# A hybrid attention layer on one core: the norm's row sent through DRAM, later places for copies and forget logits, two new banks at the end, and gate units placed anew

## Chip, core and metric

The kernel runs on one core of one Trainium2 chip. The metric is the device time of one execution in microseconds (us). TensorE is called PE here, VectorE DVE, ScalarE ACT, GpSimd POOL, and SyncE SP; SP issues most of the DMAs, and its own queue is SPq in the profile.

## What is computed

One layer over 512 frames of width 2048, in float32:

```python
hn = rmsnorm(x, norm_g)                          # x * rsqrt(mean(x*x)+eps) * g
proj = hn @ w_in                                 # 2048 -> 3*(q,k,v,gate of 512) + 4 + 3*2048
f_logit = proj[..., QKVG:QKVG+4] + b_f           # 4 forget logits a frame
gates = sigmoid(proj[..., QKVG+4:] + b_gate)     # three merge gates of width 2048
ya = forgetting_attention(rms(qa), rms(ka), va, f_logit)   # logits + c[t] - c[s], c = cumsum(log_sigmoid)
yb = chunked_relpos_attention(rms(qb), rms(kb), vb, rel_bias)
yc = stick_breaking_attention(qc, kc, vc)
ys = stack(ya, yb, yc) * silu(gate branches)
out = x + sum_n(gates_n * (ys_n @ w_up_n)) @ w_out
```

## The kernel before, in words

**Arithmetic.** A product of two float32 matrices is made of three passes in a shorter float format: each operand is split into a high part (ACT's copy, L249 in the profile) and a low part (DVE's subtraction, L253), and high*high, high*low and low*high are accumulated in a PSUM bank. The two large projections are done by a Strassen scheme with seven products (1 to 7) in place of eight; sums of weight blocks are made by DVE (L662, L668, L903 for values) and by adding DMAs that POOL issues.

**Units.** The work of PE is a list of units. A unit loads a block of weights (512 KB, SP), ACT and DVE split it (tile `w`, three buffers), and PE multiplies it with the split activations. One unit of a pair takes PE 2.8 us. First come the units of the first quad (q, k, v and gate of head C0, four banks at once), then the values of branch C (`value_units`, 14 units: product 1 in two halves, then product 2 in two halves, and so on), then head after head: `HEADS` lists for each head which units come between its q and k and the next head: `s` a pair of silu gates, `v` the 14 value units of the next branch, `g` a pair of merge gates. At the end come the up projection and the output projection (`OutTask`, twice).

**Order.** The kernel writes its instructions in an order that a planner in the kernel (`Flow`) works out while it is built. Each task is a generator that yields what it needs: an engine and a cost, an event, or a free buffer. The planner keeps one clock for each engine and always takes the task that can start first, then the one that is due first. `set_(event)` gives an event the end of the step that was placed last (`Flow.set`: `event.t = self.fin`). Data that a DMA brings is planned by `landing()`, at a rate that `line` adds up, plus 1.5; transposing DMAs by `XLATE`. On PE, ACT and DVE the order is kept as written, so an instruction whose data are late holds up all that stand behind it on its engine. SP's DMAs are kept in order too.

**The norm.** The projections run on x * g without the norm. `square_x` sums squares while x comes in; `norm_x` makes rsqrt of the mean as a column: `rcol`, 128 partitions by 4. The outputs have frames along the free dimension, so the factor is needed as a row of 512 in every partition: `rstd`, kept in `begin_in` (the buffer of the first tile of x). Before, `norm_x` makes four diagonal blocks `dg` from the identity (L527, ACT), multiplies them by a matrix of ones on PE (L532), and copies the bank to `rstd` (L536, ACT). `by_norm` (L544, DVE) multiplies a result by `rstd`. The first users are `f` (the forget logits' bank, `take_f`) and `c` (C0's v and k).

**Other places.** `forget_bias` reads the logits back as 128x64 (`lf_parts`, SP), adds them on DVE (L978) and computes log-sigmoid in short steps (L981 to L997). `Head.value` reads a head's values back from DRAM (`vr<-vd`) and splits them (`vh`, `vl`). `silu` reads a gate back. `together` copies a transposed block (`tt`) to 32-bit words (L1193, ACT). `OutTask.mms` gives PE the output products; `result` (L1846, DVE) adds a bank to the output tile `o`, which is stored. For the last unit (product 4, last quarter) the second block of rows is done in a left and a right half of 256 columns of one bank.

Of the kernel before, what the change touches and what calls it, by code (L numbers as in the profile page):

```python
# [163 lines left out]
def hybrid_kernel(  # L164
# [350 lines left out]
    def norm_x():  # L515

        m, tmp = small_n[:, 2, :], [small_n[:, i, :] for i in range(3, 6)]
        yield DVE, 0.2
        nc.vector.tensor_reduce(m, ssq, axis=AX.X, op=ALU.add)
        yield from rsqrt(rcol, m, D, tmp, 4)  # L520
        yield DVE, 0.1
        nc.vector.tensor_scalar_mul(rcol_s, rcol, SCALE)
        yield t2s, 1
        dg = t2("dg")
        for b in range(QB):
            yield ACT, 0.3
            nc.scalar.activation(dg[:, blk(b)], identf, AF.Copy, scale=rcol[:, b:b + 1])  # L527
        yield Event(flow.fin + 3.0)
        yield atts, 1
        ps = att()  # L530
        yield PE, 0.9
        nc.tensor.matmul(ps, onef, dg, start=True, stop=True)  # L532
        give(t2s, 2)
        yield begin_free
        yield ACT, act_us(S)
        nc.scalar.activation(rstd[0], ps, AF.Copy)  # L536
        give(atts)
        set_(rstd_ev)

    def by_norm(c, src=None):  # L540
# [425 lines left out]
    def forget_bias():  # L966
# [5 lines left out]
        yield f_ev  # L972
        yield from queued(nc.sync.dma_start, parts,
                          fd.rearrange("(n h) (c t) -> n (h c) t", h=NH, t=T).rearrange("n c t -> c n t"))
        yield Event(f_ev.t + 6.0)
        q = 0.15
        yield DVE, 2 * q
        nc.vector.tensor_reduce(v, parts.rearrange("p n t -> p t n"), axis=AX.X, op=ALU.add)  # L978
        nc.vector.tensor_scalar_add(v, v, bfc)
# [31 lines left out]
    class Head:  # L1011
# [249 lines left out]
        def value(self):  # L1261
            g, d = self.h // 2, self.h % 2
            task = values[self.n]
            for s in range(2):
                yield task.kept[g][s]
            for j in range(3):
                yield self.event("hl", j)
            yield t2s, 1
            t = t2("vr")
            to = t.rearrange("p (i s d) -> p i s d", i=2, s=2)  # L1270
            for s in range(2):
                ev = yield from fetch(to[:, :, s, :],
                                      task.dram[g][s].rearrange("p (i h d) -> p i h d", i=2, h=2)[:, :, d, :], 128)
            yield ev
            yield t2s, 2
            self.v = pair_of("v")
            yield from split(*self.v, t, S, self.event("v"))
            give(t2s)

        def silu(self):  # L1280

            if (self.n, self.h) in gd:
                d, ev = gd[self.n, self.h]
                yield ev
                yield t2s, 1
                g = t2("g")
                yield (yield from fetch(g, d, 256))
            else:
                yield self.event(G)
                g = self.c[G]  # L1290
                yield from by_norm(g)
# [181 lines left out]
    def first_head(n, h):  # L1473
        hd = Head(n, h)
        units.extend(first_quad(hd))
        at(OFF["fb"], forget_bias)
        value_units(n)
        gate_units()
        schedule(hd, OFF["a0"], OFF["b0"])
# [211 lines left out]
    class OutTask:  # L1691
# [94 lines left out]
        def mms(self, u):  # L1786
# [14 lines left out]
                        yield accs[i], 1  # L1801
                        self.ps[p, s] = acc(i)

            def step(s, part, cols):
                for j in range(QK):
                    k = kq * QK + j
                    yield lambda: mops[p](k) is not None
                    r, _, ev = mops[p](k)
                    yield ev
                    yield PE, mm_us(cols.stop - cols.start)  # L1810
                    w = u.lo if part == 1 else u.hi
                    mm(self.ps[p, s][:, cols], r[:, part // 2, s * P:(s + 1) * P], w[:, j, cols],
                       onto is None and kq + j + part == 0, kq == 3 and j == QK - 1 and part == 1, True)
# [14 lines left out]
            yield u.ready  # L1828
            for s in range(2):
                yield from step(s, 1, whole)  # L1830
                if kq == 3:
                    spawn(self.result(p, s, whole), 0.5, flow.fin)

        def result(self, p, s, cols):
            ps = self.ps[p, s][:, cols]
            add, sub = nc.vector.tensor_add, nc.vector.tensor_sub
            first = {1: (1, add), 5: (4, sub), 6: (2, add), 4: (3, sub)}.get(p)
            then = {2: (1, add, 1), 3: (2, add, 6), 7: (4, sub, 5)}.get(p)
            i, do = (first or then)[:2]
# [4 lines left out]
            o = self.o[i, s][:, cols]  # L1844
            yield DVE, dve_us(cols.stop - cols.start)
            do(o, o, ps)  # L1846
            if p not in (1, 5, 6, 7) and cols.stop == S:
# [6 lines left out]
            if p in (2, 3, 7, 4):  # L1854
# [73 lines left out]
    for k in range(UK):  # L1928
# [76 lines left out]
```

## Time and profile before

| | |
|---|---|
| median of 3 runs | 1296.71 us (1295.04 to 1296.72) |
| the profiled execution | 1295.77 us, its span 1294.0 us |
| PE busy | 1286.2 us, 99% of the span, 6965 matmuls |
| DVE, ACT, POOL busy | 1137.9, 873.4, 100.0 us |
| waits of PE put down to another engine | 4.4 us in 7 places |
| granted TensorE clock | full in every slice |

The sum of the waits is of the seven rows of the view of waits for PE. Since PE is busy nearly all the time, what counts of the work of the other engines is where it makes PE wait.

### The profile page before, as it was taken

The numbers are of one execution on the slowest core, as the hardware profiler recorded it, in microseconds if no ns is written. First come the engines' busy times: TensorE is split into PE (matmuls) and PEld (weight loads), VectorE is DVE, ScalarE is ACT, GpSimd is POOL, SyncE is SP. The second block draws the span as 40 slices with busy tenths as digits, with TensorE's granted clock in tenths as the row PEclk, the third lists the DMA queues.
The fourth block names the chain that finished last, engine by engine and source line by source line (L and its number), as shares of the span: only waits on it lengthen the run. The fifth ranks groups of instructions, "written<-read, shape, count | busy, mean of one in ns | idle before, by whom it ended". The sixth has DMA issues, their size and how long they took to land.

```text
span 1294.0 us, 19495 instructions
## 1 busy us (share of the span) xinstructions
PE 1286.2 (99%) x6965; PEld 1112.3 (86%) x6965; DVE 1137.9 (88%) x1666; ACT 873.4 (68%) x1359; POOL 100.0 (8%) x130
## 2 busy tenths in 40 slices
PE   9999999999999999999999999999999999999998
PEld 6888888888888888888888888888888888888887
DVE  8988889788998999989789999999899877798775
ACT  8887677777867669676857675967758655454432
POOL 0200100110010000102010000001000000000000
PEclk9999999999999999999999999999999999999999
DMA  9879898779889778878887888888988656875821
GB/s 341 235 176 253 196 243 190 218 196 228 219 209 247 179 210 199 252 201 236 219 218 200 195 232 219 195 242 194 223 212 284 228 194 194 236 218 139 255 97 65
DMA packets 130257, 274.47 MB, mean 212 GB/s; under 512 B 43104, under 2 KB 49504, under 8 KB 130160
## 3 DMA queue, kind: packets, MB, share of 16 engines
q1 hardware_dynamic: 113504, 217.19, 53.9%
q0 software_dynamic: 16224, 55.58, 25.1%
q8 instruction: 55, 0.90, 0.3%
q10 hardware_dynamic: 432, 0.45, 0.1%
q14 instruction: 42, 0.34, 0.1%
HBM read 241.54 MB, written 24.42 MB: 206 GB/s over the span
## 4 chain that ended last, share of the span: by engine, by line
PE 93%; DVE 3%; DMA 2%; ACT 1%; SPq 1%; issue 1%; ACTq 0%; DVEq 0%
PE acc L268 72%; PE att L268 17%; DVE w L253 1%; SPq L281 1%; DMA vr<-vd 1%; PE att L264 1%; PE att L265 1%; PE att L263 1%; PE att L1321 1%; PE att L1322 1%; PE att L1320 0%; DMA lf_parts<-fd 0%; ACT w L249 0%; DMA tt<-p 0%; DMA raw<-in_w_one 0%
## 5 line engine op out<-in xcount | busy, mean ns | idle before, releaser
L253 DVE TENSOR_TENSOR w<-raw,w 128x1024 fp32r<-128x1024 f32 (+2 forms) x432 | 500.3, 1165 | 90.9 <-ACT w L249 89.8
L249 ACT ACTIVATE w<-raw 128x1024 fp32r<-128x1024 f32 (+2 forms) x432 | 435.9, 1012 | 209.7 <-PE att L268 106.3
L268 PE MATMUL acc<-x,w 128*128 128x512 f32 (+1 forms) x2656 | 497.9, 339 | 0.4 <-ACT w L414 0.4
L268 PEld LDWEIGHTS acc<-x,w 128*128 128x128 f32 x2656 | 425.2, 189 | 65.9 <-issue 2.5
L268 PE MATMUL acc<-t,w 128*128 128x512 f32 (+1 forms) x1920 | 358.2, 338 | 2.3 <-ACT u L742 1.3
L268 PEld LDWEIGHTS acc<-t,w 128*128 128x128 f32 x1920 | 292.2, 190 | 36.3 <-ACT u L742 1.5
L293 POOL DMA_DIRECT2D raw<-in_w_col x80 | 68.9, 861 | 788.8 <-DMA raw<-in_w_col 265.7
L268 PE MATMUL att<-w,m 128*128 128x512 f32 (+1 forms) x342 | 94.5, 386 | 0.5 <-DVE o L1846 0.5
L268 PE MATMUL acc<-w,m 128*128 128x512 f32 x336 | 94.2, 389 | 0.0
L268 PE MATMUL att<-y,w 128*128 128x512 f32 x384 | 89.6, 389 | 0.0
L268 PEld LDWEIGHTS att<-y,w 128*128 128x128 f32 x384 | 72.1, 188 | 15.0
L268 PEld LDWEIGHTS att<-w,m 128*128 128x128 f32 x342 | 63.6, 188 | 13.7 <-DVE o L1846 0.7
L268 PEld LDWEIGHTS acc<-w,m 128*128 128x128 f32 x336 | 63.1, 188 | 13.2
L268 PE MATMUL acc<-w,x 128*128 128x512 f32 (+1 forms) x336 | 63.6, 339 | 0.0
L268 PEld LDWEIGHTS acc<-w,x 128*128 128x128 f32 x336 | 52.0, 190 | 7.1 <-DVE w L253 0.3
L544 DVE TENSOR_TENSOR c<-c,begin_in 128x512 f32<-128x512 f32 x80 | 54.0, 684 | 0.2
L662 DVE TENSOR_TENSOR raw<-raw,raw 128x1024 f32<-128x1024 f32 x40 | 48.8, 1220 | 0.4
L668 DVE TENSOR_TENSOR raw<-raw,raw 128x1024 f32<-128x1024 f32 x40 | 48.7, 1218 | 0.2
L742 ACT ACTIVATE u<-acc 128x512 f32<-128x512 f32 x43 | 25.5, 594 | 33.4 <-PE acc L268 33.2
L1548 ACT ACTIVATE sg<-sg,small_in 128x512 f32<-128x512 f32 x48 | 33.4, 715 | 21.4 <-DMA sg<-gl 21.4
L763 ACT ACTIVATE u<-acc 128x512 f32<-128x512 f32 x42 | 24.9, 592 | 33.0 <-PE acc L268 30.7
L268 PE MATMUL acc<-y,w 128*128 128x512 f32 x192 | 46.1, 389 | 0.0
(209 smaller groups left out, 1412.5 us busy)
## 6 DMA issues: line engine op xcount, KB each, us to landing
raw<-in_w_col SPq DMA_DIRECT2D x200, 512.0 KB, 4.7
raw<-in_w_col POOLq DMA_DIRECT2D x80, 512.0 KB, 7.0
raw<-in_w_v SPq DMA_DIRECT2D x24, 512.0 KB, 5.1
gl<-c SPq DMA_DIRECT2D x48, 256.0 KB, 4.3
raw<-in_w_up SPq DMA_DIRECT2D x32, 384.0 KB, 3.7
sg<-gl SPq DMA_DIRECT2D x48, 256.0 KB, 4.1
raw<-in_w_out SPq DMA_DIRECT2D x24, 512.0 KB, 4.5
raw<-in_w_v POOLq DMA_DIRECT2D x24, 256.0 KB, 7.9
```

Source lines behind the costliest of these rows:

```text
L249: nc.scalar.activation(hi, src, AF.Copy)
L253: nc.vector.tensor_sub(lo, src, f(hi))
L263: nc.tensor.matmul(ps, lh, rh, start=start, stop=False, skip_group_check=more)
L264: nc.tensor.matmul(ps, lh, rl, start=False, stop=False, skip_group_check=more)
L268: nc.tensor.matmul(ps, w, x, start=start, stop=stop, skip_group_check=more)
L293: tc.keep_in_program_order(nc.gpsimd.dma_start(to, src, accum_op=ALU.add))
L544: nc.vector.tensor_mul(c, c if src is None else src, rstd[0][:c.shape[0], :])
L662: nc.vector.tensor_add(w[1], w[1], w[5])
L668: nc.vector.tensor_add(w[2], w[2], w[1])
L742: nc.scalar.activation(self.u, ps, AF.Copy)
L763: nc.scalar.activation(self.s, ps, AF.Copy)
L1548: nc.scalar.activation(g, g, AF.Sigmoid, bias=bg[:, n * DT + d:n * DT + d + 1])
```

## The change

1. `norm_x` no longer makes `dg` and no longer uses PE. It writes `rcol` to a DRAM row `rd` of 512 floats (each of the 512 elements apart, SP), and then reads that row into `begin_in` in all 128 partitions (256 KB, SP). The read waits for the write, and both stand in SP's queue. In the planner the read is asked for 5 after the write's issue, and behind the read `norm_x` ends with `set_(rstd_ev)`.
2. `forget_bias` gets a slack of 20 and a cost of 0.21 in place of 0.15 for a step, and its event is 12 after the logits' in place of 6.
3. The data of `vr<-vd` and of the silu gate read back are planned 3 later (`SLOW`), transposed blocks 6 in place of 4 after their issue (`XLATE`).
4. In the last output unit the two halves of the second block go to two new banks. The bank that holds the first three quarters is added to `o` one unit earlier.
5. `HEADS`: one merge-gate pair is moved from behind C2's silu pair to B0, and one from B2 to B3, behind the values.

```diff
@@ norm_x
-        yield t2s, 1
-        dg = t2("dg")
-        for b in range(QB):
-            yield ACT, 0.3
-            nc.scalar.activation(dg[:, blk(b)], identf, AF.Copy, scale=rcol[:, b:b + 1])
-        yield Event(flow.fin + 3.0)
-        yield atts, 1
-        ps = att()
-        yield PE, 0.9
-        nc.tensor.matmul(ps, onef, dg, start=True, stop=True)
-        give(t2s, 2)
+        give(t2s)
+        rd = dp.tile([1, S], F32, name="rd")
+        yield from queued(nc.sync.dma_start, rd.rearrange("o (b p) -> p (o b)", p=P), rcol)
+        yield Event(flow.fin + 5.0)
         yield begin_free
-        yield ACT, act_us(S)
-        nc.scalar.activation(rstd[0], ps, AF.Copy)
-        give(atts)
+        yield (yield from fetch(rstd[0], rd.partition_broadcast(P), 256))
         set_(rstd_ev)
@@ forget_bias, first_head
-        yield Event(f_ev.t + 6.0)
-        q = 0.15
+        yield Event(f_ev.t + 12.0)
+        q = 0.21
...
-        at(OFF["fb"], forget_bias)
+        at(OFF["fb"], forget_bias, 20.0)
@@ value, silu
-            yield ev
+            yield Event(ev.t + SLOW)
...
-                yield (yield from fetch(g, d, 256))
+                ev = yield from fetch(g, d, 256)
+                yield Event(ev.t + SLOW)
@@ OutTask.mms, last unit
                 for s, cols in ((0, whole), (1, LH), (1, RH)):
-                    yield from bank(s)
+                    if s:
+                        yield atts, 1
+                        self.ps[p, s] = att()
                     for part in (0, 2, 1):
-                        yield from step(s, part, cols)
+                        yield from step(s, part, cols, s == 1 and part == 0)
...
-                if kq == 3:
+                if kq == 3 or s and self.last and (p, kq) == (4, 2):
                     spawn(self.result(p, s, whole), 0.5, flow.fin)
@@ tables
-XLATE = 4.0
+XLATE, SLOW = 6.0, 3.0
-HEADS = [(C, 1, "gg"), (C, 2, "sg"), (C, 3, "v"), (B, 0, "sggg"), (B, 1, "g"), (B, 2, "sggg"),
-         (B, 3, "gvg"), (A, 0, "sgg"), (A, 1, "gg"), (A, 2, "sggg"), (A, 3, "gggg")]
+HEADS = [(C, 1, "gg"), (C, 2, "s"), (C, 3, "v"), (B, 0, "sgggg"), (B, 1, "g"), (B, 2, "sgg"),
+         (B, 3, "gvgg"), (A, 0, "sgg"), (A, 1, "gg"), (A, 2, "sggg"), (A, 3, "gggg")]
```

What this does to the order is shown at three places. Names with numbers are tiles; `acc` and `att` are PSUM banks, `t` parts of activations, `w` a split block of weights.

The first is DVE around the end of the first quad, before: the copies of C0's k and gate out of their banks (L1417), the low part of the fifth load's weights (`w_695<-raw_547`, product 2's first half), then the first uses of `rstd` (L544).

```order
L253 TENSOR_TENSOR t_111_651<-x_359,t_111_651 128x256
L253 TENSOR_TENSOR t_100_558<-x_198,t_100_558 128x256
L1417 COPY c_692<-acc_201 128x512
L1417 COPY c_694<-att_203 128x512
L253 TENSOR_TENSOR t_110_648<-x_242,t_110_648 128x256
L253 TENSOR_TENSOR w_695<-raw_547,w_695 128x1024
L253 TENSOR_TENSOR t_113_665<-x_217,t_113_665 128x256
L544 TENSOR_TENSOR f_724<-att_126,begin_in 128x512
L544 TENSOR_TENSOR c_693<-c_693,begin_in 128x512
```

The same place of the changed kernel, where `begin_in` is what the read of the DRAM row brings:

```order
L253 TENSOR_TENSOR t_112_679<-x_213,t_112_679 128x256
L253 TENSOR_TENSOR t_100_558<-x_198,t_100_558 128x256
L535 TENSOR_TENSOR f_698<-att_126,begin_in 128x512
L1409 COPY c_688<-acc_201 128x512
L1409 COPY c_690<-att_203 128x512
L535 TENSOR_TENSOR c_689<-c_689,begin_in 128x512
L253 TENSOR_TENSOR t_109_648<-x_242,t_109_648 128x256
L253 TENSOR_TENSOR t_112_679<-x_217,t_112_679 128x256
L253 TENSOR_TENSOR t_110_651<-x_359,t_110_651 128x256
L253 TENSOR_TENSOR w_691<-raw_547,w_691 128x1024
```

The first use of `rstd` has moved ahead of the two copies and of `w_691`, and now stands where DVE is as the quad ends.

The second is SP's queue at the same time, before and after: the last loads of C's value weights (six in a row, the last two are shown), then what comes next.

```order
L281 DMA raw_555<-in_w_v 128x1024
L281 DMA raw_560<-in_w_v 128x1024
L281 DMA fd<-f_724 4x512 x2
L281 DMA gd_131<-c_693 128x512
L281 DMA fd<-f_724 4x512 x2
L281 DMA raw_861<-in_w_v 128x1024
```

And the same stretch of SP's queue in the changed kernel:

```order
L281 DMA raw_555<-in_w_v 128x1024
L281 DMA raw_560<-in_w_v 128x1024
L281 DMA rd<-small_n 128x4x1
L281 DMA begin_in<-rd 128x512
L281 DMA fd<-f_698 4x512 x4
L281 DMA gd_131<-c_689 128x512
L281 DMA raw_856<-in_w_v 128x1024
```

The write and the read of the row stand directly behind the six loads.

The third is the forget logits on DVE. Before:

```order
L253 TENSOR_TENSOR w_1202<-raw_1015,w_1202 128x1024
L978 TENSOR_REDUCE lf<-lf_parts 128x16
L979 TENSOR_SCALAR lf<-lf,small_in 128x16
L981 SCALAR_TENSOR_TENSOR lf<-lf 128x16
L253 TENSOR_TENSOR w_1230<-raw_974,w_1230 128x1024
L986 TENSOR_SCALAR lf<-lf 128x16
L987 RECIPROCAL lf<-lf 128x16
L988 TENSOR_TENSOR lf<-lf 128x16
L989 TENSOR_TENSOR lf<-lf 128x16
L990 TENSOR_SCALAR lf<-lf 128x16
L993 SCALAR_TENSOR_TENSOR lf<-lf 128x16 x6
L253 TENSOR_TENSOR w_1260<-raw_1051,w_1260 128x1024
```

After, from the same instruction on:

```order
L253 TENSOR_TENSOR w_1197<-raw_1010,w_1197 128x1024
L969 TENSOR_REDUCE lf<-lf_parts 128x16
L970 TENSOR_SCALAR lf<-lf,small_in 128x16
L972 SCALAR_TENSOR_TENSOR lf<-lf 128x16
L253 TENSOR_TENSOR w_1225<-raw_969,w_1225 128x1024
L977 TENSOR_SCALAR lf<-lf 128x16
L978 RECIPROCAL lf<-lf 128x16
L979 TENSOR_TENSOR lf<-lf 128x16
L980 TENSOR_TENSOR lf<-lf 128x16
L981 TENSOR_SCALAR lf<-lf 128x16
L984 SCALAR_TENSOR_TENSOR lf<-lf 128x16 x3
L253 TENSOR_TENSOR w_1255<-raw_1046,w_1255 128x1024
```

The reduction stands where it stood; three of the short steps have moved behind the next weights.

More of the change, by code (lines that the diff above doesn't have):

```diff
@@ L1802, in bank, with step @@
                         self.ps[p, s] = acc(i)
-            def step(s, part, cols):
+            def step(s, part, cols, opens=False):
                 for j in range(QK):
@@ L1812, in step @@
                     mm(self.ps[p, s][:, cols], r[:, part // 2, s * P:(s + 1) * P], w[:, j, cols],
-                       onto is None and kq + j + part == 0, kq == 3 and j == QK - 1 and part == 1, True)
+                       opens and j == 0 or onto is None and kq + j + part == 0, kq == 3 and j == QK - 1 and part == 1, True)
             whole = slice(0, S)
@@ L1836, in result @@
             add, sub = nc.vector.tensor_add, nc.vector.tensor_sub
+            if cols.stop - cols.start < S:
+                yield self.ev[4, 1]
             first = {1: (1, add), 5: (4, sub), 6: (2, add), 4: (3, sub)}.get(p)
@@ L1846, in result @@
             do(o, o, ps)
-            if p not in (1, 5, 6, 7) and cols.stop == S:
+            if p not in (1, 5, 6, 7) and cols == slice(0, S):
                 if s:
@@ L1853, in result @@
                 set_(self.ev[p, s])
-            if p in (2, 3, 7, 4):
+            if p in (2, 3, 7, 4) and not (self.last and p == 4 and s and cols == slice(0, S)):
                 b, c = (s, 2 + s, s, 2 + s)[i - 1], 2 * self.g + (i > 2)
```

## The prediction

> **What bounds the kernel.** I read the page's busy times and its chain first, then PE's waits, then the timeline around each place that the change touches.
>
> ```profile
> PE 1286.2 (99%) x6965; PEld 1112.3 (86%) x6965; DVE 1137.9 (88%) x1666; ACT 873.4 (68%) x1359; POOL 100.0 (8%) x130
> PE 93%; DVE 3%; DMA 2%; ACT 1%; SPq 1%; issue 1%; ACTq 0%; DVEq 0%
> ```
>
> PE is busy 99% of the span and carries 93% of the chain. So an edit counts only in two ways: PE work that goes, and waits of PE that come or go. Its waits now (engine, instruction, releaser: us in total, times, longest):
>
> ```profile
> PE acc L268 <- ACT u L742: 1.3, 1, 1.3
> PE acc L268 <- DVE v L767: 0.5, 1, 0.5
> PE att L268 <- DVE o L1846: 0.5, 1, 0.5
> PE acc L268 <- DVE w L253: 0.4, 1, 0.4
> PE att L1053 <- DVE sq L253: 0.2, 1, 0.2
> ```
>
> These five are 2.9 us, and each is one event. The other two rows lie at the start, which the change leaves alone. No repair of waits can gain more than 2.9.
>
> **The norm's row: what goes.** The timeline at the end of the first quad (start, length, what, idle time before and its releaser):
>
> ```profile
> 39.66 3.31 SPq L281 DMA_DIRECT2D raw<-in_w_v  x6
> 48.26 0.17 DVE L522 TENSOR_SCALAR small_n<-small_n 128x4 f32<-128x4 f32 x1
> 51.83 2.43 DVE L253 TENSOR_TENSOR t<-x,t 128x256 fp32r<-128x256 f32 x7
> 53.97 0.84 PE L268 MATMUL acc<-w,x 128*128 128x512 f32 x3
> 54.17 0.68 DVE L1417 COPY c<-acc 128x512 f32<-128x512 f32 x1
> 54.65 1.02 PE L532 MATMUL att<-dg,tmpc 128*128 128x512 f32 x2
> 54.77 0.68 DVE L1417 COPY c<-att 128x512 f32<-128x512 f32 x1
> 55.70 1.22 DVE L253 TENSOR_TENSOR w<-raw,w 128x1024 fp32r<-128x1024 f32 x1
> 55.71 0.60 ACT L536 ACTIVATE begin_in<-att 128x512 f32<-128x512 f32 x1 [0.17 <-PE att L532]
> 55.75 1.09 PE L268 MATMUL att<-w,x 128*128 128x512 f32 x4
> 56.87 4.43 POOL L293 DMA_DIRECT2D raw<-in_w_v  x5 [6.63 <-DMA raw<-in_w_v]
> 57.18 0.68 DVE L544 TENSOR_TENSOR f<-att,begin_in 128x512 f32<-128x512 f32 x1
> 60.46 5.74 PE L268 MATMUL acc<-w,x 128*128 128x512 f32 x32
> ```
>
> The column is ready at 48.4, the row at 56.3. L532 starts at 54.65, and the row of four at 55.75 follows it and one more matmul; three matmuls take 0.68 (53.97 to 54.65), so one takes 0.23 and L532 costs PE 0.87. Without it PE would reach product 2's first half, now at 60.46, at 59.6. The copies on ACT were not on PE's path.
>
> **The norm's row: what comes.** The write is issued at about 48.5 on the queue that holds the six loads of 39.66 to 42.97. How busy the 16 DMA engines are then (the last two columns are DMA share and GB/s), and what comparable DMAs take from issue to landing (kind, KB, median us; then for `cb` and for `vr` minimum, median, maximum):
>
> ```profile
> 52.00:54.00 2.00, 2.00 (x11) 1.65 (x10) 2.00 (x7) 1.73 (x6) 0.00 (x0) 1.00 1.09 281
> 54.00:56.00 2.00, 2.00 (x9) 1.31 (x8) 2.00 (x5) 1.83 (x4) 0.00 (x0) 1.00 0.65 131
> 56.00:58.00 2.00, 2.00 (x16) 1.87 (x15) 2.00 (x4) 1.39 (x5) 1.13 (x3) 1.00 0.02 4
> out<-o SPq DMA_DIRECT2D x15, 256.0 KB, 2.1
> fd<-lf SPq DMA_DIRECT2D x1, 8.0 KB, 4.8
> cb<-fd SPq DMA_DIRECT2D x4, 256.0 KB, 5.3
> DMA to landing us min/median/max: 4.1/5.3/6.4
> DMA to landing us min/median/max: 3.5/5.7/9.5
> ```
>
> The engines are full until 54 and empty only at 56. POOL waits until 56.87 for one of these loads. So I put the landing of the write at 56.6, as late as the loads ahead of it. The ends are 50.7 (it overtakes them, and takes 2.1 as the `out<-o` stores do, the shortest of any) and 58 (it lands last and its 512 elements take over a us). Then SP, which waits for it, needs 0.3 to issue the read. `cb<-fd` is the same read, one DRAM row into 128 partitions: 5.3, between 4.1 and the 9.5 of the slowest `vr`. The row is there at 56.6 + 0.3 + 5.3 = 62.2; the ends are 50.7 + 0.3 + 4.1 = 55.1 and 58 + 0.3 + 9.5 = 67.8.
>
> The Trainium skill, page "DMA: Bandwidth & Descriptors", section on queues, rings and completion order, says that each DMA engine takes the descriptors of a ring in order; that speaks against the change, and the rows agree in that POOL still waits for one of the six loads 14 us after the last was issued. Its section on the anatomy of one DMA gives about 2.0 us fixed and bytes/436e3 besides; an estimate from that page is 48.5 + 2.0 + 0.3 + 2.6 = 53.4 for the row, no wait at all and a gain of 0.87. The measured 4.8 and 5.3 differ from it, so they are used.
>
> DVE does not get there at 62 but at 53.9: seven parts end at 54.26, about 0.34 apart, and one of them now stands behind. From there its order is `f`, both copies, `c`, three parts, then `w_691`. The planner took the row for ready when the read was issued: `set_` gives the event the end of the last placed step, and behind the read that is SP's issue, not the landing. So all of DVE stands from 53.9 to 62.2 behind `f`. From there to the weights: four steps 0.60 apart (54.17 to 54.77), three parts of 0.34, and 1.22, together 4.6. `w_691` is done at 66.8. PE needs it for product 2 and has nothing else to do, since its order is fixed: it waits from 59.6 to 66.8, 7.2 us, and stands 66.8 - 60.46 = 6.3 behind the kernel before. The saved 0.87 is in that.
>
> Then DVE has no lead. It was busy for all but 1 us before 77:
>
> ```profile
> 60.67 0.42 DVE L253 TENSOR_TENSOR t<-x,t 128x256 fp32r<-128x256 f32 x1 [0.40 <-ACT t L249]
> 62.77 1.22 DVE L903 TENSOR_TENSOR raw<-raw,raw 128x1024 f32<-128x1024 f32 x1 [0.54 <-DMA raw<-in_w_v]
> 77.70 0.69 DVE L253 TENSOR_TENSOR w<-raw,w 128x512 fp32r<-128x512 f32 x1 [0.88 <-ACT w L249]
> ```
>
> Between `w_691` and the weights of product 6 stand two sums of weights (L903 now; 1.14 each, 1.22 less the 0.08 by which neighbours overlap), one more split (1.14), three parts, `c` and the split itself: 2.28 + 1.14 + 1.02 + 0.60 + 1.22 = 6.3, against 5.6 for PE's two units (the row of 60.46 less its tail). That is another 0.7, and the same count one product on gives 0.4 more: 1.1 in all. The lower end is 0. A second price comes in at the upper end:
>
> ```profile
> L1920 PE MATMUL att<-tmpc x19: 272/421/421, 1.1 to 4.7; 128*128 128x256 bf16 x19
> 67.85 0.64 PE L268 MATMUL acc<-w,t 128*128 128x256 f32 x4
> 68.32 0.64 PE L268 MATMUL att<-w,t 128*128 128x256 f32 x4
> ```
>
> At the start, coming from rest, 19 matmuls of 256 columns take 3.6 us; later they come 0.12 apart, which is 2.3. If a rest of 7 us does the same, 1.3 are lost, and DVE uses that time to catch up. So 0 to 2.4, and I take 1.2, which either mechanism gives alone. The Trainium skill, page "TensorE: Matmul & The Clock Gate", part 1, says that the clock is halved after an idle window of about 3.4 us; by that the second price is paid. No row shows it: the longest wait here is 1.3 us and the granted clock stays at 1.00.
>
> Sum for the norm's row: +6.3 + 1.2 = +7.5.
>
> **The repairs.** The rows of the five waits and what is late ahead of them:
>
> ```profile
> 107.39 0.26 DVE L978 TENSOR_REDUCE lf<-lf_parts 128x16 f32<-128x64 f32 x1 [3.08 <-DMA lf_parts<-fd]
> 110.31 1.23 DVE L993 SCALAR_TENSOR_TENSOR lf<-lf 128x16 f32<-128x16 f32 x6
> 657.99 0.63 ACT L249 ACTIVATE vh<-vr 128x512 fp32r<-128x512 f32 x1 [3.38 <-DMA vr<-vd]
> 919.03 1.37 ACT L1193 ACTIVATE p<-tt 128x1024 uint16<-128x1024 uint16 x1 [3.30 <-DMA tt<-p]
> 1290.02 0.62 PE L268 MATMUL att<-w,m 128*128 128x256 f32 x3 [0.52 <-DVE o L1846]
> 1288.47 0.69 DVE L1846 TENSOR_TENSOR o<-o,acc 128x512 f32<-128x512 f32 x1 [4.84 <-PE acc L268]
> ```
>
> - Forget logits: the reduction stands where it stood, so its 3.08 stay; the larger event changes nothing, since it has passed long before the unit at which the task starts. But three steps of 0.2 go behind the next weights, and DVE reaches `v` (L767) 0.6 earlier: the 0.5 goes.
> - Values: `SLOW` moves `vh` back by 3.0, against 3.38 waited: of PE's 1.3 behind it most goes.
> - Transposed blocks: 2.0 more against 3.30 waited; of the 0.4 and 0.2 I count half.
> - Two banks: PE's right half no longer waits for DVE's reading of the left, 0.5 gone. The extra sum of 512 columns lies in DVE's 4.84 idle.
> - The gate units do the same work in another place: 0 in themselves. They move what lies beside each head's scores, so new waits can come; the five old ones average 0.6, and I allow one.
>
> 0.5 + 1.2 + 0.3 + 0.5 - 0.1 = 2.4 gained if the new wait is a small one; the ends are 0 and 2.9.
>
> **Sum.** 1295.8 (profiled) + 7.5 - 2.4 = 1300.9. The median of the runs is 0.9 above the profiled execution: 1301.8.
>
> **Rivals.**
>
> 1. The write overtakes the loads and lands at 50.7, and the read takes the shortest 4.1: the row is there at 55.1, `w_691` at 59.7, PE waits 0.1. The change then gains 0.8 + 2.4: 1293.5, faster. For it: 16 bytes a partition are little. Against it: full engines until 54, and POOL's wait. It decides below a row at 56: there `w_691` comes at 60.6, and the norm's part gains nothing.
> 2. The write lands at 54, when most engines are through, and the read is fast: 58.4, +2.5 and no more behind it: 1296.8, no change.
> 3. The row is late, and so is the rest: the read meets POOL's five adding loads (issued from 56.87) and takes up to 9.5, or both prices behind the wait fall due, or the moved gate units bring new waits that eat the 2.4: 1304.6 to 1310. For it: the DMA share was about full before and the five loads go out just then.
> 4. The repairs do not do what they say, because a later place in the planner's order is only taken where something else is ready: 1304.2 with the norm's part as forecast, which lies in the forecast's own range and is counted there.
>
> **How the numbers follow.** A change within 0.2% (2.6 us) can hardly be told from none here. Forecast, a row between 60 and 65: 0.58, 1299.6 to 1304.6. Rival 1: 0.09. Rival 2: 0.16. Rival 3: 0.17. From these: faster 0.09, within 0.2% 0.16, slower 0.75. The range 1297.3 to 1307 leaves out the first rival, some of the second and the far end of the third; the forecast's own range is 1299.6 to 1304.6.
>
> **What the profile after would show.** DVE idle for some 8 us ahead of `f` (L535) at about 54, released by the DMA into `begin_in`, and SP's read issued near 57. PE waiting about 7 us near 60, released by DVE's `w`; the granted clock below 1.00 in that slice if the rest halves it. At the end no wait of PE for L1842, and ACT hardly waiting for `vr<-vd`. I am wrong if the row lands before 56, if DVE has something else to do ahead of `f`, or if the moved units cost PE more than the five waits.

## The result

The changed kernel takes 1316.0 us (median of 5 runs, 1310.7 to 1318.9) against 1296.7 for the kernel before. The ratio is 1.0152, 95% interval 1.0125 to 1.0179: slower by 19.7 us by that ratio. The forecast was 1301.8, with a range up to 1307.0. The sign was right, the size was not. The profiled execution took 1315.5, its span 1313.7.

The chain's shares by engine, and PE's waits (engine, instruction, releaser: us in total, times, longest), in the profile after:

```profile
PE 93%; DMA 4%; DVE 1%; ACT 1%; issue 1%; SPq 0%; DVEq 0%; POOLq 0%
```

```profile
PE acc L268 <- DVE w L253: 17.9, 4, 13.0
PE acc L268 <- ACT w L249: 0.4, 1, 0.4
PE acc L268 <- DVE v L758: 0.2, 1, 0.2
```

The waits for `u`, `v` of 0.5, `o` and `sq` that the prediction listed are gone or smaller. One instruction, the split of weights on DVE, now keeps PE waiting for 17.9 us in four places, 13.0 of them in one. That one is at the norm's row. The timeline there (start, length, what, idle time before and its releaser; DVE's, PE's, POOL's and SP's rows together):

```profile
48.72 0.40 SPq L281 DMA_DIRECT2D rd<-small_n  x1
55.74 4.43 POOL L293 DMA_DIRECT2D raw<-in_w_v  x5 [6.76 <-DMA raw<-in_w_v]
61.01 0.33 SPq L281 DMA_DIRECT2D begin_in<-rd  x1
68.43 0.69 DVE L535 TENSOR_TENSOR f<-att,begin_in 128x512 f32<-128x512 f32 x1 [14.04 <-DMA begin_in<-rd]
73.20 7.11 PE L268 MATMUL acc<-w,x 128*128 128x512 f32 x28 [13.04 <-DVE w L253]
```

The write is issued at 48.7, as forecast. The read that waits for it goes out only at 61.0. The row is there at 68.4, DVE has stood at `f` for 14.0 us, and PE for 13.0. Then comes a second price. The windows of the profile after (us; busy time and count of PE, PEld, DVE, ACT and POOL; granted clock, DMA share, GB/s):

```profile
54.00:56.00 2.00, 2.00 (x10) 1.68 (x9) 0.39 (x2) 2.00 (x4) 0.26 (x1) 1.00 0.66 99
56.00:58.00 2.00, 2.00 (x17) 1.93 (x16) 0.00 (x0) 0.89 (x2) 2.00 (x5) 1.00 0.91 33
58.00:60.00 2.00, 2.00 (x11) 1.48 (x9) 0.00 (x0) 1.68 (x4) 2.00 (x3) 1.00 0.12 16
60.00:62.00 2.00, 0.17 (x1) 0.00 (x0) 0.00 (x0) 1.42 (x3) 0.16 (x1) 1.00 0.84 49
...
68.00:72.00 4.00, 0.00 (x0) 0.00 (x0) 3.57 (x8) 0.00 (x0) 0.00 (x0) 0.50 0.74 147
72.00:76.00 4.00, 2.80 (x7) 2.25 (x8) 4.00 (x6) 1.06 (x1) 0.00 (x0) 0.50 0.13 49
```

After the rest the clock is at half: PE's first 28 matmuls take 7.11 us. By the trace's records the 25th starts 6.0 us behind the first, and before it was 3.7, so 2.3 are lost. The first four windows show something that the prediction did not look for: between 56 and 62 the DMA engines count as busy or idle by turns, but hardly any bytes move (16 to 49 GB/s, where it was 383 to 397 between 48 and 52, while loads ran).

A second place lies in the values of branch B, where the kernel before had no wait. First SP's rows before, then the timeline after:

```profile
237.25 6.66 SPq L281 DMA_TRANSPOSE tt<-z  x5
246.34 6.43 SPq L281 DMA_DIRECT2D raw<-in_w_v  x4
```

```profile
253.06 7.71 SPq L281 DMA_TRANSPOSE tt<-z  x6
261.86 4.44 POOL L293 DMA_DIRECT2D raw<-in_w_v  x5 [11.27 <-DMA raw<-in_w_v]
267.59 1.23 DVE L894 TENSOR_TENSOR raw<-raw,raw 128x1024 f32<-128x1024 f32 x1 [6.39 <-DMA raw<-in_w_v]
270.01 2.07 PE L268 MATMUL acc<-w,t 128*128 128x512 f32 x4 [3.04 <-DVE w L253]
...
610.47 4.26 PE L268 MATMUL acc<-w,x 128*128 128x512 f32 x25 [0.69 <-DVE w L253]
```

Before, the transposing DMAs of head C3's logits were through when SP issued all but the first of the value weights. After, they go out behind the value weights and among POOL's adding loads. DVE waits 6.4 us for the data of a sum of weights (L894), PE waits 3.0, and the clock is halved there too. Near 605 to 610, in the values of branch A, PE waits 0.4, 1.1 and 0.7, at full clock.

### The profile page after: what moved, and what is told of

Its sections match the earlier page's. It is cut to its first block, busy times and chain, and to the rows that moved or that the text cites. A ratio compares the mean times of both kernels' runs of the same rounds, so it can differ in the third digit from the quotient of the medians.

```text
span 1313.7 us, 19483 instructions
## 1 busy us (share of the span) xinstructions
PE 1290.7 (98%) x6963; PEld 1116.4 (85%) x6963; DVE 1137.6 (87%) x1667; ACT 873.5 (66%) x1354; POOL 100.0 (8%) x130
## 4 chain that ended last, share of the span: by engine, by line
PE 93%; DMA 4%; DVE 1%; ACT 1%; issue 1%; SPq 0%; DVEq 0%; POOLq 0%
PE acc L268 73%; PE att L268 16%; DMA raw<-in_w_v 2%; DVE w L253 1%; PE att L264 1%; PE att L1313 1%; PE att L1314 1%; PE att L265 1%; DMA begin_in<-rd 1%; PE att L263 1%; PE att L1312 1%; DMA lf_parts<-fd 0%; DMA tt<-p 0%; ACT w L249 0%; DMA raw<-in_w_one 0%
## 5 line engine op out<-in xcount | busy, mean ns | idle before, releaser
L268 PE MATMUL acc<-w,x 128*128 128x512 f32 (+1 forms) x336 | 65.0, 346 | 13.7 <-DVE w L253 13.7
L653 DVE TENSOR_TENSOR raw<-raw,raw 128x1024 f32<-128x1024 f32 x40 | 48.7, 1218 | 0.2
```

What stands on the lines that cost most here:

```text
L268: nc.tensor.matmul(ps, w, x, start=start, stop=stop, skip_group_check=more)
L653: nc.vector.tensor_add(w[1], w[1], w[5])
```

## The experiments

My first theory was read off this trace: three sums that do not touch each other, the norm's row +14.5, the moved gate units +8.8, the repairs -3.8. The first four kernels undo one part or do one part alone.

**e1: the changed kernel with the old norm.**

```diff
-        rd = dp.tile([1, S], F32, name="rd")
-        yield from queued(nc.sync.dma_start, rd.rearrange("o (b p) -> p (o b)", p=P), rcol)
...
+            nc.scalar.activation(dg[:, blk(b)], identf, AF.Copy, scale=rcol[:, b:b + 1])
...
+        nc.tensor.matmul(ps, onef, dg, start=True, stop=True)
```

> The changed kernel with the old way of the norm's row (diagonal blocks, PE, ACT's copy); everything else as changed. Theory: three sums that do not touch each other, the norm's row +14.5 us (13.0 of waiting, 2.3 of half clock behind it, less 0.87 of removed PE work), the moved gate units +8.8 (waits and half clock near 266 and near 604), the repairs -3.8. Then 1316.0 - 14.5 = 1301.5: PE's wait of 13 us near 60 is gone, the ones near 266 and 604 stay. Rival: the later waits are an aftermath of the first (PE and the loads are shifted against each other by 13 us): then they go as well, 1292.9.

**e2: the changed kernel with the gate units as before.**

```diff
-HEADS = [(C, 1, "gg"), (C, 2, "s"), (C, 3, "v"), (B, 0, "sgggg"), (B, 1, "g"), (B, 2, "sgg"),
-         (B, 3, "gvgg"), (A, 0, "sgg"), (A, 1, "gg"), (A, 2, "sggg"), (A, 3, "gggg")]
+HEADS = [(C, 1, "gg"), (C, 2, "sg"), (C, 3, "v"), (B, 0, "sggg"), (B, 1, "g"), (B, 2, "sggg"),
+         (B, 3, "gvg"), (A, 0, "sgg"), (A, 1, "gg"), (A, 2, "sggg"), (A, 3, "gggg")]
```

> The changed kernel with the gate units where they were; the row through DRAM and the repairs as changed. Theory (three separate sums): 1316.0 - 8.8 = 1307.2; PE still waits 13 us near 60, and has no wait of more than 0.5 near 266 and 604. Rivals: the waits there come from the later planned places of copies and blocks, or are an aftermath of the first wait; by either they stay, 1316.

**e3: both undone, so that only the repairs are left.** Its edit is those of e1 and e2 together.

> Only the repairs: later planned places of what transfers feed, forget logits later, two new banks at the end; norm and gate units as before. Theory: 1296.7 - 3.8 = 1292.9, and no wait of PE over 0.5 behind the start. The prediction's own sum for them is -2.4: 1294.3. Rival (the waits near 266 and 604 come from the later planned places, not from the gate units): 1296.7 + 8.8 - 3.8 = 1301.7.

**e4: the kernel before with the new norm alone.** Its edit is that of e1 the other way round.

> The kernel before with the norm's row through DRAM alone. Theory: 1296.7 + 14.5 = 1311.2, with PE waiting 13 us near 60 at a half clock behind it, and the old five small waits in place. Rival (the later waits are an aftermath of this one): 1320, with waits in B's value units also here. The prediction's sum for this part was +7.5: 1304.2.

Measured:

| | median us | ratio to before | 95% interval | in us |
|---|---|---|---|---|
| changed | 1316.0 | 1.0152 | 1.0125 to 1.0179 | +19.7 |
| e1 without the row | 1301.7 | 1.0038 | 1.0025 to 1.0051 | +4.9 |
| e2 without the moved units | 1310.6 | 1.0115 | 1.0092 to 1.0137 | +14.9 |
| e3 repairs alone | 1297.3 | 1.0010 | 1.0000 to 1.0020 | +1.3 |
| e4 row alone | 1310.2 | 1.0105 | 1.0090 to 1.0120 | +13.6 |

The last column is the ratio less 1, times 1296.6. The row alone costs 13.6, and with the rest around it 14.8 (changed less e1) or 13.6 (e2 less e3). The moved units cost 4.8 (changed less e2) or 3.6 (e1 less e3), the repairs 1.3. The row alone, the units beside the repairs and the repairs alone come to 13.6 + 3.6 + 1.3 = 18.5, against 19.7 for all together; the interval of the changed kernel's time is 16.2 to 23.2, so the parts add up as far as can be told. e1 and e4 came out as the theory said, but its other two terms were wrong: the moved units cost half of what the one profile showed (and the clock near 604 was full, which the theory had otherwise), and the repairs gained nothing. In e2 PE's wait near 60 stayed (11.4) and the waits in the value units went, but for 0.3 and 0.2 near 610, so they belong to the moved units; new ones of 0.9 and 0.8 stand at 348 and 365, and the old one for `v`, now 0.7, at 126. In e1 the value units' wait stays, without a half clock behind it:

```profile
254.97 1.20 PE L268 MATMUL acc<-w,t 128*128 128x512 f32 x4 [2.41 <-DVE w L253]
```

These four matmuls take 1.20 here and 2.07 in the changed kernel. So the clock fell in the one profiled execution and not in the other, and the moved units' price with it. The length of the wait alone does not decide that, as the last section shows. e3's waits of PE:

```profile
PE acc L268 <- DVE w L253: 2.1, 4, 1.1
PE att L1925 <- POOL nhepsc L325: 1.1, 1, 1.1
PE acc L268 <- DVE v L767: 0.2, 1, 0.2
```

The five old waits are gone here too, but for 0.2 of the one for `v`, and 2.1 of new ones stand in their place, at 350, 594 and 1154. The other runs of e3 took 1 to 4 us more than the profiled one (1294.8), and no profile shows where. Nor does the forget logits' later place always end the wait for `v`: e1, e2, e15 and e16 have it too, and there that wait is 0.7, where it was 0.5 before.

**Why the row is late: four kernels.** All start from e4. In e7 the planner is told the truth, so that DVE's order has 21 other instructions ahead of `f`. In e8 the write has a queue to itself. In e9 it has fewer and larger pieces, and the right order of the frames is left out. e11 is e7 and e9 together, and leaves that out too.

```diff
@@ e7
         yield from queued(nc.sync.dma_start, rd.rearrange("o (b p) -> p (o b)", p=P), rcol)
+        asked = flow.fin
...
-        yield (yield from fetch(rstd[0], rd.partition_broadcast(P), 256))
-        set_(rstd_ev)
+        yield from fetch(rstd[0], rd.partition_broadcast(P), 256)
+        rstd_ev.t = asked + 20.0
@@ e8
-        yield from queued(nc.sync.dma_start, rd.rearrange("o (b p) -> p (o b)", p=P), rcol)
+        yield ACT, 0.4
+        tc.keep_in_program_order(nc.scalar.dma_start(rd.rearrange("o (b p) -> p (o b)", p=P), rcol))
@@ e9
-        yield from queued(nc.sync.dma_start, rd.rearrange("o (b p) -> p (o b)", p=P), rcol)
+        yield from queued(nc.sync.dma_start, rd.rearrange("o (p b) -> p (o b)", p=P), rcol)
```

> The kernel before with the norm's row through DRAM (as in e4), but the planner is told that the row is there 20 us after its write is issued, so that DVE gets other work ahead of the first use: the copies, five splits of weights and three sums now stand ahead of `f`. Theory (what costs is only that DVE's fixed order has the late row ahead of `w`): PE's wait near 60 and the half clock are gone, 1296.6 - 0.9 = 1295.7. Rival (the two DMAs themselves cost, since they push back the loads behind them, or a bank stays taken): new waits of 2 to 4 us between 60 and 80, 1299.

> As e4, but ACT issues the write of the row on its own queue, so that it does not stand behind the six loads in SP's. Theory A (queueing behind the loads makes the write late): it lands some 5 us after its issue, near 53.5, the row is there near 60, PE waits about 5 in place of 12.5: 1302.5. Theory B (512 elements of 4 bytes are slow in themselves while the engines are full, in whatever queue): it lands near 59 as before, 1310.

> As e4, but each partition writes its four factors as 16 bytes in one piece: 128 pieces in place of 512. The factors then stand at the wrong frames of the row, so the scaling leaves out the right order of frames; sizes and work are the same. Theory A (the 5 us from the write's last packet to its landing are a price of the many small pieces): it lands near 57 in place of 59.9, PE waits 9 in place of 12.5, 1306.5. Theory B (the landing waits for the engines, which POOL's adding loads hold): it lands at 59 to 60 as before, 1310.

> e7 (row's uses planned late) with the write in 128 pieces of 16 bytes in place of 512 of 4; the factors stand at the wrong frames, so the scaling leaves out the right order. Theory (512 small writes hold up the other transfers too: in e7 POOL's adding loads came late and DVE waited 2.8 for one, PE 1.9): POOL's load of the time lands near 55.5 in place of 60, no wait of PE near 65, 1298.4 - 2.0 = 1296.4. Rival (that wait is due to the read of 256 KB amid the adding loads): it stays, 1298.4.

| | median us | ratio to before | 95% interval | PE's wait near 60 to 68 |
|---|---|---|---|---|
| e7 late uses | 1298.4 | 1.0021 | 1.0012 to 1.0030 | 1.9 |
| e8 write on ACT's queue | 1307.8 | 1.0085 | 1.0068 to 1.0102 | 10.0 |
| e9 pieces of 16 bytes | 1304.9 | 1.0071 | 1.0053 to 1.0090 | 7.4 |
| e11 e7 and e9 | 1295.6 | 0.9997 | 0.9985 to 1.0010 | none over 0.2 |

The last column explains the times of the kernels in which DVE stands before `f`. In e4 the wait is 12.5: with 2.1 for the half clock, taken as above from the 25th matmul, less the 0.87 of L532, that is 13.7, and 13.6 were measured. The same sum gives 10.0 + 2.2 - 0.87 = 11.3 for e8 (measured 11.0) and 7.4 + 2.5 - 0.87 = 9.0 for e9 (9.2). For e7 it gives 1.0, and 2.7 were measured; the rest stays open.

The DMAs of the row in the changed kernel, in e8 and in e9 (kind, KB, median us from issue to landing):

```profile
raw<-in_w_v POOLq DMA_DIRECT2D x2, 512.0 KB, 10.6
...
rd<-small_n SPq DMA_DIRECT2D x1, 2.0 KB, 12.1
```

```profile
rd<-small_n ACTq DMA_DIRECT2D x1, 2.0 KB, 11.3
```

```profile
rd<-small_n SPq DMA_DIRECT2D x1, 2.0 KB, 7.5
begin_in<-rd SPq DMA_DIRECT2D x1, 256.0 KB, 6.4
```

And the packets of the write in the records of the trace, with the landing beside them (us):

```
                        pieces   first starts   last ends   landed
changed, SP's queue   512 x  4 B  51.4 to 52        56.0     60.9
e8, ACT's queue       512 x  4 B         52.0        59.6     60.0
e9, SP's queue        128 x 16 B         52.0        55.1     55.6
```

Not every 4-byte packet there is a piece of the row: e8's queue has 528 for 512 pieces, and in the changed kernel those of the loads stand among them. So the last end is the latest that a piece can have; e9's are told apart by their size.

So the queue was not what made the write late. On ACT's queue, where nothing stands ahead, it also moved nothing before 52, when the loads were nearly through, and it landed at the same 60. With 128 pieces the last packet was 0.9 us earlier than in the changed kernel, and the landing came 0.5 us behind it, with 512 pieces 4.9 us behind. In e4, from which e9 starts, the last packet ended at 55.1 as in e9, and the landing came at 59.9. In e8 some 500 of the queue's 4-byte packets were through by 53.5 and the last came at 59.6. The sizes of the pieces decide: theory A of e9, theory B of e8. e8 waits 2.5 us less than e4 all the same: DVE's new order has both copies, 1.2 us, ahead of `f`, and the read was 0.8 us shorter.

The Trainium skill, page "DMA: Bandwidth & Descriptors", gives 512 bytes in its table of specifications as the least transfer for full rate, and says that a smaller one is read, modified and written back. The runs agree in the direction: behind the last packet, 2 KB in 512 pieces take 4.4 us more than in 128. Whether reading back is the mechanism no run here shows.

The small pieces also held up the others. e7 had its uses late enough, and DVE never waited for the row, but:

```profile
65.04 1.22 DVE L895 TENSOR_TENSOR raw<-raw,raw 128x1024 f32<-128x1024 f32 x1 [2.81 <-DMA raw<-in_w_v]
```

```profile
67.45 1.20 PE L268 MATMUL acc<-w,t 128*128 128x512 f32 x4 [1.93 <-DVE w L253]
```

A load of weights that has nothing to do with the row is 2.8 late there, and PE waits 1.9 for it. In e11, with 16 bytes, that wait is gone. So e7 met its rival, and e11 its theory.

**e13: four rows of 512 bytes.** It starts from e7. PE turns the column into four rows first, which keeps the order of the frames.

```diff
+        rrow = cp.tile([QB, P], F32, name="rrow")
+        yield Event(flow.fin + 3.0)
+        yield atts, 1
+        ps = att()
+        yield PE, 0.1
+        nc.tensor.transpose(ps[:QB, :P], rcol, identf)
+        yield ACT, 0.3
+        nc.scalar.activation(rrow, ps[:QB, :P], AF.Copy)
+        give(atts)
-        yield from queued(nc.sync.dma_start, rd.rearrange("o (b p) -> p (o b)", p=P), rcol)
+        yield from queued(nc.sync.dma_start, rd.rearrange("o (b p) -> (o b) p", p=P), rrow)
...
+        rstd_ev.t = asked + 14.0
```

> The kernel before with the norm's row through DRAM, but PE first turns the column into four rows of 128, ACT copies them, and the write has 4 pieces of 512 bytes; the row's uses are planned late. A version that could beat both. Theory (small pieces and the place of the first use are all that is wrong with the way through DRAM): no wait of PE over 0.5 between 55 and 80, 1296.6 - 0.9 + 0.2 = 1295.9. Rival (the write still stands behind the six loads and the read among the adding loads): DVE or PE waits 1 to 3 there, 1298.

It took 1295.2, ratio 0.9987, interval 0.9978 to 0.9996. The write went out at 53.1 and the read at 55.4, so the write took at most 2.3 us:

```profile
53.07 0.32 SPq L281 DMA_DIRECT2D rd<-rrow  x1
55.37 0.35 SPq L281 DMA_DIRECT2D begin_in<-rd  x1
```

```profile
raw<-in_w_v POOLq DMA_DIRECT2D x2, 512.0 KB, 7.7
...
begin_in<-rd SPq DMA_DIRECT2D x1, 256.0 KB, 4.5
```

The row was there at 59.8, 8.6 us sooner than in the changed kernel, and POOL's loads of the same stretch took 7.7 where they take 10.6 there. The write was also issued 5 us later than in the other kernels, when the loads ahead of it were nearly through, and the read went out just ahead of POOL's five adding loads (55.67), not behind them; no run separates these from the size of the pieces.

**e17: the changed kernel, all of it, with e13's row.**

> The changed kernel, all of it, with the row written in four pieces of 512 bytes and its uses planned late (as in e13). Theory (small pieces and the place of the first use are the whole price of the row, the moved gate units and the later places the rest): 1301.7 (e1) - 0.7 = 1301, PE's waits near 250 and 590 stay, none of over 1 near 60. Rival (something else of the change makes the row dear): over 1305.

It took 1300.5, ratio 1.0035 (1.0021 to 1.0048), as e1 with the old norm did. So within the changed kernel as well, the way the row is written and the place of its first use are the whole price of the row. PE's waits near 250 and 590 stayed.

**The moved units: e5.** It is e3 with only the pair from C2 moved to B0.

```diff
-HEADS = [(C, 1, "gg"), (C, 2, "sg"), (C, 3, "v"), (B, 0, "sggg"), (B, 1, "g"), (B, 2, "sggg"),
+HEADS = [(C, 1, "gg"), (C, 2, "s"), (C, 3, "v"), (B, 0, "sgggg"), (B, 1, "g"), (B, 2, "sggg"),
```

> e3 (only the repairs) with one of the two moved gate pairs, the one from C2 to B0. Theory (each pair takes away the cover of one set of value units: without it the transposing DMAs of C3's logits fall among the loads and adding loads of B's values): PE waits 2 to 3 us near 252, none over 0.6 near 590; 1297.3 + 3 = 1300. Rival (the waits come from both together, or from chance): no wait over 1 near 252, 1297.

1299.2, ratio 1.0024 (1.0013 to 1.0035), and the wait is at the place that the theory names:

```profile
254.29 1.56 PE L268 MATMUL acc<-w,t 128*128 128x512 f32 x4 [2.30 <-DVE w L253]
```

Near 600 the longest wait is 0.3, as in e3. So the pair from C2 makes the wait near 250. The other pair was not moved alone: e1, which has both, shows 0.7 at 590 and took 1.8 us more than e5 by the ratios, whose intervals overlap. I read it so that each pair had stood between the transposes of one head and the loads of the next values. That the transposes among the loads delay them is read from the order of the rows; no run moved the transposes alone.

**The repairs: e12, e15, e16.** e3 gained nothing where 2.4 were forecast. These take away one or both of the later planned places.

```diff
@@ e12
-XLATE, SLOW = 6.0, 3.0
+XLATE, SLOW = 4.0, 0.0
@@ e15
+XLATE, SLOW = 4.0, 3.0
@@ e16
+XLATE, SLOW = 6.0, 0.0
```

> e3 without the later planned places (no SLOW, transposed blocks planned at 4 as before): of the repairs only the forget logits and the two banks are left. Theory (the later places end their own waits, 1.3 + 0.4 + 0.2, and bring as much in new ones): 1296 to 1297, with the waits near 657 and 920 back and none near 350 and 594. Rival (they cost more than they end): 1295.6, the kernel before less 0.5 for each of the two that are left.

> e3 with the later place of the copies and gates read back (SLOW 3), but transposed blocks planned at 4 as before. e3 took 1297.3, without both later places 1295.3 (e12). Theory (it is the 6 for transposed blocks that costs, since it puts DVE's and ACT's work on them behind that of the next weights): 1294.5, the wait near 657 gone and none near 350. Rival (SLOW costs): 1297.

> e3 with transposed blocks planned at 6, but no SLOW. Theory (the 6 costs the 2): 1297.3, waits near 350 and 594 as in e3 and the one near 657 back. Rival (SLOW costs them): 1295.

| XLATE, SLOW | median us | ratio to before | 95% interval |
|---|---|---|---|
| 4, 0 (e12) | 1295.3 | 0.9986 | 0.9978 to 0.9995 |
| 4, 3 (e15) | 1297.2 | 1.0009 | 1.0000 to 1.0018 |
| 6, 0 (e16) | 1299.7 | 1.0028 | 1.0016 to 1.0039 |
| 6, 3 (e3) | 1297.3 | 1.0010 | 1.0000 to 1.0020 |

e12 came out as its rival: without the later places the repairs gain 0.14%, though the wait near 657 is back. Each of the later places alone costs, and together they cost no more than SLOW alone. e15 took the time of its rival, yet the 6 costs as well: e16 took 2.4 more than its theory. So this is no sum of two prices. The waits of the profiled executions show what moved. e15's longest new one, then e16's:

```profile
PE att L1053 <- DVE sq L253: 1.7, 2, 1.3
```

```profile
PE acc L268 <- ACT u L742: 2.1, 1, 2.1
```

In e15 the wait for `u` near 657 is gone, and one of 1.3 for `sq` near 595 has come, in another head. In e16 the wait for `u` of 1.3 has moved to another head, near 329, and become 2.1. I read this so that a planned time 2 or 3 us later puts the later steps in another order, and the waits fall where the new order has them. That is argued from one profile each; why they fall just there stays open.

**The candidates for a better version: e10 and e14.** e10 is e7 with the repairs; e14 is e13 with the two repairs that e12 has.

> As e7, with the repairs of the change (later planned places, two new banks) and the gate units as before: the candidate for a version that beats both. If the parts add up as their comparisons so far gave them, 1295.7 + 0.7 = 1296.4, no change against the kernel before; if the repairs gain what their profiled execution showed (-1.0 in the profiled time) and the row costs nothing, 1294.7.

> The kernel before with the norm's row through DRAM in four pieces of 512 bytes (e13) and with two of the repairs, forget logits and two banks (e12): the candidate for a version that beats both. Theory (the parts add up: -1.4 of e12, -1.5 of e13): 1293.8. Rival (each of the two gains is the same 1 to 1.5 us of chance in the places of the loads): 1295.3.

e10 took 1298.4, ratio 1.0019 (1.0007 to 1.0031); the small pieces cost it a wait of 2.8 near 65. e14 took 1295.7, ratio 0.9998 (0.9989 to 1.0007). So the gains of e12 and e13, 0.14% and 0.13%, are not a sum either: together they give none, as e14's rival had it. Both may be luck of the order, of the size that any new order brings here. No version was found that beats the kernel before by more than 0.2%.

## Why the prediction was wrong in size

- **PE without L532.** PE began to wait at 73.20 - 13.04 = 60.16; forecast 59.6. Right to 0.6.
- **DVE stands behind `f`, and all else behind DVE.** Right, with its cause, the event that is set at the read's issue: forecast from 53.9, measured from 68.43 - 14.04 = 54.39. e7 and e17 showed it: with the event late, DVE does not wait for the row.
- **The landing of the write, 56.6, with 58 as the upper end.** This step failed first. It landed at 60.9. The prediction took the loads ahead for what binds, and counted "over a us" for the 512 elements. The loads were indeed through at 55, and POOL's wait ended at 55.74. But from the last small packet to the landing it took 4.9 more, and e8 and e9 show that the pieces, not the queue, are what mattered. The order in a ring, which the prediction weighed, was thus beside the point; the size of the pieces was what bore on it, and it had no term but that "over a us". (The estimate of 53.4 beside the sum goes by a fit that the Trainium skill, page "DMA: Bandwidth & Descriptors", anatomy of one DMA, gives for DMAs issued by GpSimd; SP issues both of these. The sum did not use it.)
- **The read, 5.3.** 7.4: within the ends. With larger pieces it took 6.4 (e9), 4.6 (e11) and 4.5 (e13), but the place differs too: in e11 and e13 it went out 0.2 to 0.3 us ahead of POOL's five adding loads, in e9 0.7 behind the first of them, and in the changed kernel 5.3 behind. e8, with small pieces and 0.7 behind, took 6.3, like e9, and e17, 1.2 ahead, took 3.1. So the meeting with POOL's loads, which the third rival named, fits the times better than the size of the pieces; no run separates the two. The row came at 68.4, past the upper end of 67.8.
- **From the row to the weights, 4.6.** PE started 4.8 after DVE did. Right. PE's wait became 13.0 in place of 7.2, by the lateness of the row alone.
- **The price behind the wait, 1.2 (0 to 2.4).** 2.3 (2.1 in e4), and it is the half clock, not DVE without lead: PE has no further wait there. The Trainium skill, page "TensorE: Matmul & The Clock Gate", part 1, was right that a rest halves the clock.
- **Sum of the row, +7.5.** Measured +13.6 to +14.8, of which 6.2 are the row's lateness (5.0 in e4) and 1 the clock.
- **The moved gate units, 0.1.** This step failed too: 3.6 to 4.8. The prediction gave one new wait of the average size of the old ones. But those were what was left in the old placing. What a moved unit uncovers is not of that size: 3.0 and a half clock in one place, three waits in the other.
- **The repairs, -2.4.** In the changed kernel's profile the five waits went, but for 0.2. The net is +1.3 (0 to 2.6). The step that failed is that the sum counted what each repair ends and nothing for what its later places bring: without SLOW and the later XLATE the repairs gain 1.8 (e12), and with them they lose 1.3. The rival "the repairs do not do what they say" named another reason and is not what happened.
- **The chances.** The third rival (a later row, the price behind the wait at its upper end, new waits from the moved units) is what came, but all three together. They were priced as one or the other, up to 1310. Added, with the row at 67.8 (5.6 later), that price at 2.4 (1.2 more) and no gain of the repairs, they give 1296.7 + 7.5 + 5.6 + 1.2 = 1311.0.

## What to carry over

The column written to DRAM as 512 pieces of 4 bytes was no small DMA, though it holds 2 KB: it landed 12.1 us after its issue, and in e13, turned first into four pieces of 512 bytes, at most 2.3 after. So count pieces, not bytes. When a planner sets the order on engines that run in order, look at what time its event really gets; the first use planned too early cost 13.0 us of waiting here, and 1.9 were left once it was planned 20 behind the write. And do not sum the gains of repairs of single waits in a kernel that is 99% busy: here each change of a planned time moved waits of 1 to 2 us to other places, so repairs of that size have to be measured together.

## What had not been expected of the hardware

With the 512 writes of 4 bytes the transfers of other queues were slow for some 5 us. The load that POOL issued at 48.1 in the changed kernel took 11.6 and landed at 59.7; in e9 the same load, issued at 47.1, took 8.3 and landed at 55.4, and in the kernel before it took 7.9. The single packets of 4 KB of POOL's loads between 55 and 62 took up to 4.7 us each in the changed kernel, and up to 1.5 in e9 (median 0.6 and 0.3). The longest began at 57.9, before the read of the row went out at 61.0, so the read is not what held them up.

The rest that halves the clock is short, and its length alone does not decide. The windows of e10 behind a wait of 2.8 us, and those of e17 behind one of 2.9 (2.95 by the starts of its matmuls):

```profile
68.00:70.00 2.00, 1.75 (x8) 1.44 (x9) 1.93 (x5) 1.19 (x2) 0.00 (x0) 1.00 1.10 201
```

```profile
256.00:258.00 2.00, 2.00 (x9) 1.81 (x8) 2.00 (x5) 2.00 (x3) 0.00 (x0) 0.50 1.03 217
```

The one stays at 1.00 and the other falls to 0.50. In e17 it falls only 1.5 us after PE has started again. But in e5 it also fell, to 0.50 from 255 to 258, behind a wait of 2.30, which is shorter than those of e10 (2.78) and e1 (2.41) that left it full. The second four matmuls behind the wait, in e5 and in e1:

```profile
255.65 1.91 PE L268 MATMUL att<-w,t 128*128 128x512 f32 x4
```

```profile
256.00 1.08 PE L268 MATMUL att<-w,t 128*128 128x512 f32 x4
```

Nor is it the same in each execution of one kernel: of e5's ten, five had a mean granted clock of 1.000 and took 1297.8 to 1298.9, and five had 0.997 to 0.999 and took 1299.5 to 1303.7. In the trace's records of the clock, the stretches at half clock last 3.41 (e5, e17), 6.83 and 13.65 (the changed kernel) and 10.24 us (e8, e9), all whole multiples of 3.41 (but for the last, which the end cuts off), and so are the stretches between them. Cut into steps of 3.41 us from its first change of clock on, each trace shows how long PE rested in each step (us), and the clock in the next step:

| | rest of PE in the step | clock in the next |
|---|---|---|
| e1, at 253 | 1.52 | full |
| e10, at 64 | 1.76 | full |
| e7, at 66 | 1.84 | full |
| e17, at 253 | 1.89 | half |
| changed, at 266 | 2.20 | half |
| e5, at 252 | 2.30 | half |

No step of any trace here breaks that order: with 1.84 or less the full clock stayed, with 1.89 or more it fell, and it came back only behind a step without any rest. So it matters how a wait is divided by that grid, and not only how long it is. The Trainium skill, page "TensorE: Matmul & The Clock Gate", part 1, gives about 3.4 for its window, which runs freely, so that the moment varies; the grid and the delay in e17 agree with that. By the Trainium skill's table there the clock falls after a whole window of rest, but here 1.89 of 3.41 us were enough. A wait behind which the clock falls costs twice: in the changed kernel the first four matmuls behind the wait of 3.04 at 270 took 2.07, and behind e1's wait of 2.41 they took 1.20.
